# Whole low parts in the feed-forward networks, a third pair in seven products, and later small tables in a two-layer trunk

## The chip, the cores and the metric

The kernel runs on one core of a Trainium2 chip. The metric is the time on the device in microseconds (us), the median of several runs. The names of the engines are those of the profile: PE is TensorE (matrix products), PEld its loading of weights, DVE is VectorE, ACT is ScalarE, POOL is GpSimd and SP is SyncE, which here only starts transfers (DMAs).

## What is computed

A decoder trunk of two layers, forward over 256 positions (one batch) of width 2048, in float32. Layer 0 mixes by an mLSTM (8 heads) beside a Mamba-2 scan (32 heads), with one projection in front of both and one behind; layer 1 mixes by block-sparse attention. Behind each mixer stands a SwiGLU network with 5632 hidden units. Cut to what matters:

```python
def swiglu(x, w_gate, w_up, w_down):
    return (jax.nn.silu(x @ w_gate) * (x @ w_up)) @ w_down

for layer in range(DEPTH):
    xn = rms_norm(x, norm_mix[layer])
    if layer % 2 == 0:
        x = x + mixer_mlstm_ssd(xn, *mixer_params[layer])
    else:
        x = x + mixer_moba(xn, *mixer_params[layer])
    x = x + swiglu(rms_norm(x, norm_ffn[layer]), *ffn_params[layer])
return rms_norm(x, final_norm)
```

## The kernel before, in words

**High and low parts.** To keep the accuracy of float32, each weight and each activation is split in two: a high part, which ScalarE makes by a cast to the matmul's format (line 441, `wh`), and a low part, what is left, which VectorE makes by a subtraction (line 443, `wl`). Each product of a 128x128 block of activations with a 128x512 block of weights is three matmuls: high by high (line 475), activation high by weight low (line 476), and activation low by weight high (line 477). Line 476 alone needs `wl`. In the mixer's projections the same is done in the lines 383 and 387 from the splits of lines 367 and 368.

**Blocks.** `block` computes 256 tokens by 1024 columns, over pairs of 128 rows of the weight. One pair is one *unit* of weights: a DMA of 512 KB on SyncE's queue into `raw`, 128 partitions by 4x512 numbers. `weights` casts and subtracts a unit in two halves of 128x1024. A string says of each pair how it is computed: P is a plain pair, 8 products or 24 matmuls; S is a pair *in seven products* (a Strassen form), 21 matmuls. For S, VectorE also makes sums of weights (lines 450, 451 and 453, into `sums`), which are split as a second unit, and only three quarters of the raw unit are split (128x1536). Sums of activations (`sk`) are made by `sums_of`. The matmuls of one S pair go over the banks `acc_f` (four results) and `acc_e` (the products that several results share).

**The feed-forward network.** `ffn` makes 11 strips of 512 hidden units in groups of 4, 4 and 3. `hidden` makes a strip: a block of gate and up columns, then Silu (line 1011), the product (line 1012), and 128x128 transposes of the strip on TensorE. Some strips are first copied by a DMA from GpSimd's queue into `hr`, a tile in the matmul's format, and transposed from there (line 282); the others are transposed as plain float32 (line 284). Behind each group come two blocks of `w_down` (`add_blocks`, the halves q of the columns), whose plans are in `PLAN_H`; their results are added to the residual (line 909). The network of layer 0 is a, that of layer 1 is b, so `ha` and `hb` are their hidden units.

**Order.** The kernel is written operation by operation, and a scheduler places each on its engine by priority (`high_priority` with an offset) and by what it needs; `issue_after` ties one to another. Steps that are put off, transposes and parts of the mixer, go into a list with a number of steps to wait (`later`, `transpose_later`), and `tick` runs what is due behind a product. An engine then carries out its instructions in the order in which they stand. Units are staged in rings of three buffers each for `raw`, `wh` and `wl`, with an extra `raw`.

**The start.** `keep_busy(11)` gives TensorE 11 small matmuls of float32, which the profile shows as 22, until the first x and the first weights are there. x comes in features by tokens on SyncE's queue (`first_x`, `xraw`), the first two 128-row blocks of weights as two transfers, one from ScalarE's queue and one from SyncE's. Small tables (`ident`, `pv`, `alog`, `gbias`, `d_bc`, `mask_sl`) come from GpSimd's queue, and `cw_rows` from ScalarE's. Further on in the mixer, gate columns are transposed into `p_cols` (line 690).

Of the kernel before, what the change touches and what calls it, by code (L numbers as in the profile page):

```python
# [9 lines left out]
F32 = mybir.dt.float32  # L10
# [7 lines left out]
P = 128  # L18
# [22 lines left out]
PLAN_H = {4: ("PSPSPPPP", "PSPSPSPP"), 3: ("PSPSPP", "PSPSPP")}  # L41
# [24 lines left out]
def hybrid_trunk(ctx: ExitStack, tc: tile.TileContext, a: dict, out: bass.AP):  # L66
# [121 lines left out]
    keep_busy(11)  # L188
# [15 lines left out]
    nc.gpsimd.dma_start(alog[32:64], col1(a["l0_ssd_a_log"]))  # L204
    ident_r = cst.tile([P, P], F32R, name="ident_r")
    ident = ident_r.bitcast(F32)
    ident_in = t2([P, P], "ident_in")
    nc.gpsimd.dma_start(ident_in, a["ident"])
    nc.gpsimd.dma_start(ident, ident_in)
# [11 lines left out]
    def split(h, l, src, gain=None):  # L221
        if gain is None:
            nc.scalar.copy(h, src)
            nc.vector.tensor_sub(l, src, h.bitcast(F32))
        else:
            nc.scalar.activation(h, src, AF.Copy, scale=gain)
            nc.vector.scalar_tensor_tensor(l, src, gain, h.bitcast(F32), op0=OP.mult, op1=OP.subtract)
# [124 lines left out]
    def chunks(w, col, nk, first=KC):  # L352

        n = 4 if staging else KC
        for k in range(0, nk, KC):
# [4 lines left out]
            step = KC if k else first  # L360
            for i in range(0, KC, step):
                ks = slice(k % n + i, k % n + i + step)
                eng = nc.scalar if step < KC and i == 0 else nc.sync
                eng.dma_start(raw[:, ks, :],
                              w[(k + i) * P:(k + i + step) * P, col:col + STRIP].rearrange("(a p) f -> p a f", p=P))
                with tc.high_priority(offset=800):
                    nc.scalar.copy(wh[:, ks, :], raw[:, ks, :])  # L367
                    nc.vector.tensor_sub(wl[:, ks, :], raw[:, ks, :], wh[:, ks, :].bitcast(F32))  # L368
            ks = slice(k % n, k % n + KC)
            yield k, wh[:, ks, :], wl[:, ks, :]  # L370

    def lin_w(w, col, kt, nk, ready=None):
# [5 lines left out]
        for k0, wh, wl in chunks(w, col, nk, KC if ready is None else 1):  # L378
# [49 lines left out]

    def weights(src, row, summed):
# [7 lines left out]
        def parts(of, cuts):  # L437
# [4 lines left out]
            for c in cuts:  # L442
# [121 lines left out]

    def input_ready(k, last):

        if k % 2 == 0 and k < KD:
            if k == 0:
                nc.gpsimd.dma_start(pv, a["columns"])
            if k + 2 < KD:  # L570
                load_x(k + 2)
            for j in (k, k + 1):
                h, l = xt0.block(k // 4)[:, j % 4, 0, :], xt0.block(k // 4)[:, j % 4, 1, :]
                with tc.high_priority(offset=750 if j > 1 else 2000):
                    x = first_x[:, KD + j * T:KD + (j + 1) * T] if j < KC else xraw[2 * k // KD][:, j % (KD // 2), :]
                    split(h, l, x, first_x[:, j:j + 1])
# [3 lines left out]
    banks_q = lin_w(w_in, C_Q, xt0, KD, ready=input_ready)  # L580
# [3 lines left out]
    for t in range(NT):  # L584
        nc.gpsimd.dma_start(xin[t], x_in[t * P:(t + 1) * P, :])
    gbias = cst.tile([96, 1], F32, name="gbias")
    nc.gpsimd.memset(gbias, 0.0)
    nc.gpsimd.dma_start(gbias[0:8], col1(a["l0_mlstm_gate_bias"][8:16]))
    nc.gpsimd.dma_start(gbias[32:64], col1(a["l0_ssd_dt_bias"]))
    nc.gpsimd.dma_start(gbias[64:72], col1(a["l0_mlstm_gate_bias"][0:8]))  # L590
    d_bc = cst.tile([P, SH], F32, name="d_bc")
    dsrc = a["l0_ssd_d"]
    nc.gpsimd.dma_start(d_bc, bass.AP(tensor=dsrc.tensor, offset=dsrc.offset, ap=[[0, P], [1, SH]]))
    mask_sl = cst.tile([P, P], F32, name="mask_sl")
    nc.gpsimd.dma_start(mask_sl, a["mask_sl"])
# [4 lines left out]
    with tc.issue_after(emptied[1].ins):  # L600
        nc.vector.tensor_scalar(convw, cw_rows, 0.5, None, op0=OP.mult)
        nc.vector.tensor_scalar(convb, pv[:, G_CB:G_CB + 32], 0.5, None, op0=OP.mult)
# [4 lines left out]
    with tc.issue_after(emptied[0].ins):  # L607
        nc.scalar.activation(lam, alog, AF.Exp)
# [614 lines left out]
```

## Time and profile before

| what | value |
|---|---|
| median of 3 runs | 2559.82 us (2558.21 to 2562.22) |
| the profiled execution | 2558.07 us |
| its span | 2556.3 us |
| granted TensorE clock, mean | 0.999 |
| TensorE busy | 99% of the span, 12179 matmuls |
| VectorE busy | 85%, 2679 instructions |
| ScalarE busy | 57% |
| GpSimd busy | 2% |
| DMA | 509.58 MB, mean 199 GB/s |

In the timeline a row is: start, duration, engine, line, operation, output from inputs, shape, and how many such are in the row; a bracket gives the idle time ahead and what ended it. In a table of waits a row says which engine waited at which output for what: us in total, times, the longest. In groups by line, a row has the busy time, the mean of one in ns, and the idle time just ahead with what ended it. Matmuls overlap with the next one, so what counts is the distance of their starts and not their duration.

### The profile page before, as it was taken

The numbers are of one execution on the slowest core, as the hardware profiler recorded it, in microseconds if no ns is written. First come the engines' busy times: TensorE is split into PE (matmuls) and PEld (weight loads), VectorE is DVE, ScalarE is ACT, GpSimd is POOL, SyncE is SP. The second block draws the span as 40 slices with busy tenths as digits, with TensorE's granted clock in tenths as the row PEclk, the third lists the DMA queues.
The fourth block names the chain that finished last, engine by engine and source line by source line (L and its number), as shares of the span: only waits on it lengthen the run. The fifth ranks groups of instructions, "written<-read, shape, count | busy, mean of one in ns | idle before, by whom it ended". The sixth has DMA issues, their size and how long they took to land.

```text
span 2556.3 us, 32504 instructions
## 1 busy us (share of the span) xinstructions
PE 2541.2 (99%) x12179; PEld 2129.6 (83%) x12179; DVE 2176.5 (85%) x2679; ACT 1465.2 (57%) x1940; POOL 59.7 (2%) x112
## 2 busy tenths in 40 slices
PE   9999999999999999999999999999999999999998
PEld 8888888888888888888888888888888888888887
DVE  5776778798989998999899987767999988998898
ACT  6465665566556554555455655666665545564554
POOL 1000010000000000000000000000000000000000
PEclk9999999999999999999999999999999999999999
DMA  8665576566565666566656556554556756575754
GB/s 281 181 209 185 165 231 185 167 204 214 181 214 182 217 212 202 200 222 216 196 200 212 196 172 230 165 165 149 196 184 213 234 177 222 198 239 167 236 190 165
DMA packets 257774, 509.58 MB, mean 199 GB/s; under 512 B 16232, under 2 KB 16512, under 8 KB 257104
## 3 DMA queue, kind: packets, MB, share of 16 engines
q1 hardware_dynamic: 249952, 483.20, 58.0%
q0 software_dynamic: 6224, 21.56, 2.4%
q10 hardware_dynamic: 1440, 2.75, 0.3%
q8 instruction: 95, 1.56, 0.2%
q14 instruction: 63, 0.52, 0.1%
HBM read 494.76 MB, written 2.14 MB: 194 GB/s over the span
## 4 chain that ended last, share of the span: by engine, by line
PE 94%; DVE 3%; issue 1%; DMA 1%; ACT 1%; SPq 0%; POOLq 0%; POOL 0%; DVEq 0%; ACTq 0%
PE acc_f L475 19%; PE acc_f L476 18%; PE acc_f L477 18%; PE acc_w L383 11%; PE acc_w L387 6%; PE acc_e L475 4%; PE acc_e L477 4%; PE acc_e L476 4%; PE acc_a L413 2%; PE acc_a L414 2%; PE acc_a L415 2%; PE p_y L872 1%; PE p_tr L284 1%; DVE wl L443 1%; DMA raw<-in_l_w_o 1%
## 5 line engine op out<-in xcount | busy, mean ns | idle before, releaser
L441 ACT CAST wh<-raw 128x1024 fp32r<-128x1024 f32 (+1 forms) x573 | 628.6, 1137 | 496.7 <-PE acc_f L477 384.1
L443 DVE TENSOR_TENSOR wl<-raw,wh 128x1024 fp32r<-128x1024 f32 (+1 forms) x573 | 745.8, 1327 | 119.2 <-ACT wh L441 115.8
L475 PE MATMUL acc_f<-wh,x 128*128 128x512 f32 x1122 | 438.6, 391 | 0.5 <-DVE xres L909 0.5
L477 PE MATMUL acc_f<-wh,x 128*128 128x512 f32 x1122 | 436.9, 389 | 0.0
L476 PE MATMUL acc_f<-wl,x 128*128 128x512 f32 x1122 | 436.6, 389 | 0.0
L368 DVE TENSOR_TENSOR wl<-raw,wh 128x1024 fp32r<-128x1024 f32 (+1 forms) x225 | 271.0, 1217 | 130.5 <-ACT wh L367 126.8
L441 ACT CAST wh<-sums 128x1024 fp32r<-128x1024 f32 x230 | 234.8, 1051 | 199.7 <-PE acc_f L477 137.4
L367 ACT CAST wh<-raw 128x1024 fp32r<-128x1024 f32 (+1 forms) x225 | 231.7, 1044 | 184.4 <-PE acc_w L383 94.4
L443 DVE TENSOR_TENSOR wl<-sums,wh 128x1024 fp32r<-128x1024 f32 x230 | 273.6, 1219 | 11.9 <-ACT wh L441 11.7
L477 PEld LDWEIGHTS acc_f<-wh,x 128*128 128x128 f32 x1122 | 210.6, 188 | 44.1
L475 PEld LDWEIGHTS acc_f<-wh,x 128*128 128x128 f32 x1122 | 210.6, 188 | 43.8 <-issue 0.9
L476 PEld LDWEIGHTS acc_f<-wl,x 128*128 128x128 f32 x1122 | 210.6, 188 | 43.0
L383 PE MATMUL acc_w<-xa,wh 128*128 128x512 f32 x768 | 207.9, 398 | 2.9 <-ACT wh L367 1.9
L383 PEld LDWEIGHTS acc_w<-xa,wh 128*128 128x128 f32 x768 | 139.2, 189 | 29.1 <-ACT wh L367 3.3
L450 DVE TENSOR_TENSOR sums<-raw 128x1024 f32<-128x1024 f32 x115 | 140.2, 1219 | 23.0 <-DMA raw<-in_l_ffn_up 11.3
L383 PE MATMUL acc_w<-x,wh 128*128 128x512 f32 x512 | 139.2, 399 | 0.0
L387 PE MATMUL acc_w<-xa,wl 128*128 128x256 f32 x768 | 121.1, 282 | 0.0
L387 PEld LDWEIGHTS acc_w<-xa,wl 128*128 128x128 f32 x768 | 109.6, 190 | 6.5
L383 PEld LDWEIGHTS acc_w<-x,wh 128*128 128x128 f32 x512 | 92.4, 189 | 16.9
L475 PE MATMUL acc_f<-wh,hb 128*128 128x512 f32 (+1 forms) x272 | 105.1, 387 | 0.0
L477 PE MATMUL acc_f<-wh,hb 128*128 128x512 f32 (+1 forms) x272 | 105.1, 386 | 0.0
L476 PE MATMUL acc_f<-wl,hb 128*128 128x512 f32 (+1 forms) x272 | 105.1, 386 | 0.0
(354 smaller groups left out, 4567.9 us busy)
## 6 DMA issues: line engine op xcount, KB each, us to landing
raw<-in_l_w_in SPq DMA_DIRECT2D x191, 512.0 KB, 3.7
raw<-in_l_ffn_gate SPq DMA_DIRECT2D x176, 512.0 KB, 3.9
raw<-in_l_ffn_up SPq DMA_DIRECT2D x176, 512.0 KB, 4.8
raw<-in_l_ffn_down SPq DMA_DIRECT2D x176, 512.0 KB, 5.1
raw<-in_l_w_qkv SPq DMA_DIRECT2D x96, 512.0 KB, 4.6
raw<-in_l_w_out SPq DMA_DIRECT2D x64, 512.0 KB, 5.1
raw<-in_l_w_o SPq DMA_DIRECT2D x32, 512.0 KB, 4.7
hr<-h POOLq DMA_DIRECT2D x40, 256.0 KB, 4.0
```

Of the source, the lines that this page charges most:

```text
L367: nc.scalar.copy(wh[:, ks, :], raw[:, ks, :])
L368: nc.vector.tensor_sub(wl[:, ks, :], raw[:, ks, :], wh[:, ks, :].bitcast(F32))
L383: return nc.tensor.matmul(banks[f], wh[:, kk, f * P:(f + 1) * P], kt.both(k0 + kk), start=k0 + kk == 0, stop=False, skip_group_check=True)
L387: nc.tensor.matmul(banks[f][:, :T], wl[:, kk, f * P:(f + 1) * P], kt.parts(k0 + kk)[0], start=False, stop=k0 + kk == nk - 1, skip_group_ch ...
L413: nc.tensor.matmul(banks[t], xh[:, ts], wh[:, kk, :], start=k0 + kk == 0, stop=False)
L414: nc.tensor.matmul(banks[t], xh[:, ts], wl[:, kk, :], start=False, stop=False)
L441: nc.scalar.copy(h[:, c, :], of[:, c, :])
L443: nc.vector.tensor_sub(l[:, c, :], of[:, c, :], h[:, c, :].bitcast(F32))
L450: nc.vector.tensor_sub(sums[:, 0:2, :], raw[:, 2:4, :], raw[:, 3:0:-2, :])
L475: nc.tensor.matmul(dst, ah, bh, start=start, stop=False)
L476: nc.tensor.matmul(dst, ah, bl, start=False, stop=False)
L477: nc.tensor.matmul(dst, al, bh, start=False, stop=stop)
```

## The change

**A third S pair.** The plan of the first down block behind a group of four strips, one of "PSPSPPPP", becomes "PSPSPSPP". There are two such blocks in each network. The sums of activations for that pair are made three steps earlier.

**Whole low parts.** Within `ffn` a unit's low part is one subtraction of 128x2048 (128x1536 for the raw unit of an S pair, as before) in place of two of 128x1024; the casts stay in halves. That is 264 units.

**The last strip of a group** is never copied by GpSimd: 8 copies fewer, and 32 transposes go from line 282 to line 284. They are due one step sooner.

**The start.** One idle matmul fewer; ScalarE casts the first x, then the first weights, then the second x, then the second weights, and the subtractions of the weights come behind both. The small tables and `cw_rows` are loaded by GpSimd's queue behind the large loads of x in rows (`xin0`, `xin1`). What is worked out from them (`convw`, `convb`, `lam`) is done behind the second strip of q.

**The mixer.** The gate columns' transposes are put off by four steps, the adding of the mask to the decay rows by two.

The core of the diff:

```diff
-PLAN_H = {4: ("PSPSPPPP", "PSPSPSPP"), 3: ("PSPSPP", "PSPSPP")}
+PLAN_H = {4: ("PSPSPSPP", "PSPSPSPP"), 3: ("PSPSPP", "PSPSPP")}
...
-    keep_busy(11)
+    keep_busy(10)
...
+            if k == 0 and lead is not None:
+                for i, eng in enumerate((nc.scalar, nc.sync)):
+                    eng.dma_start(raw[:, i, :], rows[:, i, :])
+                with tc.high_priority(offset=2000):
+                    for i in range(KC):
+                        with tc.issue_after(cast.ins) if i else nullcontext():
+                            xh, xl = lead(i)
+                        with tc.issue_after(xh.ins):
+                            cast = nc.scalar.copy(wh[:, i, :], raw[:, i, :])
+                with tc.high_priority(offset=800), tc.issue_after(xl.ins):
+                    for i in range(KC):
+                        nc.vector.tensor_sub(wl[:, i, :], raw[:, i, :], wh[:, i, :].bitcast(F32))
...
-            for c in cuts:
+            for c in (slice(0, cuts[-1].stop),) if whole_lows[0] else cuts:
                 nc.vector.tensor_sub(l[:, c, :], of[:, c, :], h[:, c, :].bitcast(F32))
...
-    nc.scalar.dma_start(cw_rows, a["conv_w_columns"])
+    with tc.issue_after(xin_loads[0].ins):
+        nc.gpsimd.dma_start(cw_rows, a["conv_w_columns"])
+        nc.gpsimd.dma_start(pv, a["columns"])
+        nc.gpsimd.dma_start(alog[32:64], col1(a["l0_ssd_a_log"]))
+        nc.gpsimd.dma_start(ident_in, a["ident"])
+    with tc.issue_after(xin_loads[1].ins):
+        nc.gpsimd.dma_start(ident, ident_in)
...
+    later(4, "cols", turn_cols)
...
+            later(2, ("hm", s), masked, mrows[0])
...
         first = 0
+        whole_lows[0] = True
         for n in (4, 4, 3):
             hT = KT(f"h{name}{first}", 4 * n)
-            hT.sums = summed(PLAN_H[n][0])
+            hT.sums = {1: None, 3: None}
             for i in range(n):
-                hidden(hT, i, first + i, PLAN_X if first + i else PLAN_LATE, n == 4 or i < n - 1)
+                hidden(hT, i, first + i, PLAN_X if first + i else PLAN_LATE, i < n - 1)
...
-                       ahead=(((5, sums_of, hT, 5, False),) if n == 4 else (), ()))
+                       ahead=(((2, sums_of, hT, 5, False),) if n == 4 else (), ()))
             first += n
+        whole_lows[0] = False
```

Three places at which the order moves. The first is TensorE's queue in the last down block of network b, at its first S pair (banks `acc_e` and `acc_f`; a number behind a name is that of the tile, and `wl` has the number of its `wh` and one more). Before:

```order
L477 MATMUL acc_f_20678<-wh_20710,skh_20037 128x512
L475 MATMUL acc_e_20727<-wh_20710,hb80_20020 128x512
L476 MATMUL acc_e_20727<-wl_20711,hb80_20020 128x512
L477 MATMUL acc_e_20727<-wh_20710,hb80_20020 128x512
L475 MATMUL acc_e_20731<-wh_20715,skh_20037 128x512
L476 MATMUL acc_e_20731<-wl_20716,skh_20037 128x512
L477 MATMUL acc_e_20731<-wh_20715,skh_20037 128x512
```

Now, at the same place (the lines 475, 476 and 477 have become 480, 481 and 482, and the tiles have other numbers):

```order
L482 MATMUL acc_e_20470<-wh_20454,hb80_19780 128x512
L480 MATMUL acc_e_20474<-wh_20459,skh_19797 128x512
L480 MATMUL acc_e_20478<-wh_20459,skh_19797 128x512
L480 MATMUL acc_e_20482<-wh_20459,skh_19797 128x512
L480 MATMUL acc_f_20435<-wh_20459,hb80_19780 128x512
L480 MATMUL acc_f_20422<-wh_20492,hb81_20099 128x512
L480 MATMUL acc_e_20470<-wh_20527,hb81_20099 128x512
L481 MATMUL acc_e_20474<-wl_20460,skh_19797 128x512
```

Before, each product's three matmuls stand together. Now six matmuls that need a high part alone stand ahead of the first that reads the low part `wl_20460`; `wh_20492` is the next plain unit, and `wh_20527` the next S unit.

The second is VectorE's queue at that place. Before:

```order
L443 TENSOR_TENSOR wl_20711<-raw_20704,wh_20710 128x1536
L453 TENSOR_TENSOR sums_20707<-raw_20704,sums_20707 128x512
L443 TENSOR_TENSOR wl_20716<-sums_20707,wh_20715 128x1024
L443 TENSOR_TENSOR wl_20750<-raw_20746,wh_20749 128x1024
L443 TENSOR_TENSOR wl_20716<-sums_20707,wh_20715 128x1024
L443 TENSOR_TENSOR wl_20750<-raw_20746,wh_20749 128x1024
L450 TENSOR_TENSOR sums_20782<-raw_20779 128x1024
```

Now:

```order
L458 TENSOR_TENSOR sums_20451<-raw_20448,sums_20451 128x512
L1176 TENSOR_TENSOR xres0_4817<-xres0_4817,gf_20159 128x512
L455 TENSOR_TENSOR sums_20524<-raw_20521 128x1024
L1176 TENSOR_TENSOR xres1_4818<-xres1_4818,gf_20159 128x512
L448 TENSOR_TENSOR wl_20460<-sums_20451,wh_20459 128x2048
L448 TENSOR_TENSOR wl_20493<-raw_20489,wh_20492 128x2048
L456 TENSOR_TENSOR sums_20524<-raw_20521,sums_20524 128x512
```

Before, halves of the two units alternate, and the sum for the next S pair comes behind them. Now each low part is one row, and that sum and two additions of the output's residual stand ahead of the first.

The third is GpSimd's queue at the start. Before:

```order
L203 MEMSET alog_129 64x1
L208 DMA ident_in_133<-in_ident 128x128
L204 DMA alog_129<-in_l0_ssd_a_log 32x1
L213 MEMSET mhalf_136 128x16
L569 DMA pv_126<-in_columns 128x128
L587 MEMSET gbias_378 96x1
L593 DMA d_bc_383<-in_l0_ssd_d 128x32
```

Now, from the first load of x in rows on:

```order
L591 DMA xin0_368<-in_x 128x2048
L600 DMA cw_rows_376<-in_conv_w_columns 128x128
L601 DMA pv_125<-in_columns 128x128
L602 DMA alog_128<-in_l0_ssd_a_log 32x1
L603 DMA ident_in_377<-in_ident 128x128
L591 DMA xin1_369<-in_x 128x2048
L605 DMA ident_r_130<-ident_in_377 128x128
```

The tables, which stood at the queue's head, now stand behind `xin0` and `xin1`.

More of the change, by code (lines that the diff above doesn't have):

```diff
@@ L1 @@
-from contextlib import ExitStack
+from contextlib import ExitStack, nullcontext
 import numpy as np
@@ L350, in row_norm, with chunks @@
         return r, rb
[L352 removed]
+    def chunks(w, col, nk, lead=None):
         n = 4 if staging else KC
@@ L359, in chunks @@
                 wl = unit("wl", [P, n, STRIP], "wl", F32R)
[L360 to L365, printed above, removed]
+            rows = w[k * P:(k + KC) * P, col:col + STRIP].rearrange("(a p) f -> p a f", p=P)
+            ks = slice(k % n, k % n + KC)
+            if k == 0 and lead is not None:
[10 more added lines that the diff above has]
+                        nc.vector.tensor_sub(wl[:, i, :], raw[:, i, :], wh[:, i, :].bitcast(F32))
+            else:
+                nc.sync.dma_start(raw[:, ks, :], rows)
                 with tc.high_priority(offset=800):
@@ L563, in hybrid_trunk, with split_x, first_pair @@
     ss0 = cst.tile([P, NT, 4], F32, name="ss0")
+    def split_x(j, x):
+        return split(xt0.block(j // 4)[:, j % 4, 0, :], xt0.block(j // 4)[:, j % 4, 1, :], x, first_x[:, j:j + 1])
+    def first_pair(j):
+        return split_x(j, first_x[:, KD + j * T:KD + (j + 1) * T])
     def input_ready(k, last):
         if k % 2 == 0 and k < KD:
-            if k == 0:
-                nc.gpsimd.dma_start(pv, a["columns"])
             if k + 2 < KD:
                 load_x(k + 2)
[L572 to L576, printed above, removed]
+            for j in range(max(k, KC), k + 2):
+                with tc.high_priority(offset=750):
+                    split_x(j, xraw[2 * k // KD][:, j % (KD // 2), :])
     qT = long([P, MH, T], "qT")
     kT = long([P, MH, T], "kT")
-    banks_q = lin_w(w_in, C_Q, xt0, KD, ready=input_ready)
+    banks_q = lin_w(w_in, C_Q, xt0, KD, input_ready, first_pair)
     for f in range(4):
@@ L617, in hybrid_trunk @@
                 emptied = lin_sum(banks[f], qT[:, 4 + f, :])
+            with tc.issue_after(emptied[1].ins):
+                nc.vector.tensor_scalar(convw, cw_rows, 0.5, None, op0=OP.mult)
+                nc.vector.tensor_scalar(convb, pv[:, G_CB:G_CB + 32], 0.5, None, op0=OP.mult)
+            with tc.issue_after(emptied[0].ins):
+                nc.scalar.activation(lam, alog, AF.Exp)
+            with tc.issue_after(emptied[1].ins):
+                nc.vector.tensor_scalar(lam, lam, -1.0, None, op0=OP.mult)
             continue
```

54 lines of the change are left out of this document (22 added, 32 removed).

## The prediction

> **What bounds the kernel now.** First the profile page's busy shares and its chain of waits:
>
> ```profile
> PE 2541.2 (99%) x12179; PEld 2129.6 (83%) x12179; DVE 2176.5 (85%) x2679; ACT 1465.2 (57%) x1940; POOL 59.7 (2%) x112
> PE 94%; DVE 3%; issue 1%; DMA 1%; ACT 1%; SPq 0%; POOLq 0%; POOL 0%; DVEq 0%; ACTq 0%
> ```
>
> TensorE (PE) is the bound: busy 99% of the span, 94% of the chain that ended last. VectorE (DVE), at 85%, has the least room of the rest. So I read next what TensorE waits for, which is all that an edit elsewhere could win:
>
> ```profile
> PE acc_w L383 <- ACT wh L367: 1.9, 1, 1.9
> PE p_idle L186 <- POOL alog L203: 1.0, 1, 1.0
> PE acc_w L383 <- DVE xa L227: 1.0, 1, 1.0
> PE acc_f L475 <- DVE xres L909: 0.5, 1, 0.5
> PE p_cols L690 <- ACT colsrc L681: 0.4, 1, 0.4
> PE p_tr L284 <- DVE pre L528: 0.3, 1, 0.3
> ```
>
> These six waits are 5.1 us of 2556. Little is to be won by hiding things; time moves by TensorE's own work, and by new waits. The profiled execution took 2558.07 us (span 2556.3); the median of three runs is 2559.82. I sum against the former and add the difference, 1.75, at the end. A measurement of this kernel can tell about 0.2%, some 5.1 us, from no change.
>
> **Third pair in seven products.** The order shows 2637 matmuls for each of lines 475 to 477 where there were 2641: four blocks each lose one product, 3 matmuls, so 12. Their pitch:
>
> ```profile
> 2520.13 0.39 PE L475 MATMUL acc_f<-wh,hb 128*128 128x512 f32 x1
> 2522.17 0.39 PE L475 MATMUL acc_e<-wh,skh 128*128 128x512 f32 x1
> ```
>
> Nine matmuls start from 2520.13 to 2522.17, 0.227 us each, so 12 give **-2.7**. [...]
>
> VectorE pays for it. One such block before, and the costs of its operations:
>
> ```profile
> 966.80:1009.00 42.20, 42.20 (x188) 34.94 (x188) 34.71 (x33) 19.00 (x19) 0.00 (x0) 1.00 0.51 162
> L443 DVE TENSOR_TENSOR wl<-raw,wh 128x1024 fp32r<-128x1024 f32 x458 | 546.5, 1219 | 103.2 <-ACT wh L441 100.4
> L443 DVE TENSOR_TENSOR wl<-raw,wh 128x1536 fp32r<-128x1536 f32 x115 | 201.6, 1753 | 16.0 <-ACT wh L441 15.4
> L453 DVE TENSOR_TENSOR sums<-raw,sums 128x512 f32<-128x512 f32 x115 | 78.8, 685 | 1.0
> ```
>
> The window's columns after the length are the busy times of PE, weight loads, DVE, ACT, POOL. A plain pair has two subtractions of 1.22. A pair in seven products has one of 1.75, a sum of 1.22, two of 0.69, and two more subtractions of 1.22: about 4.3 us more, 4.0 where neighbours overlap. VectorE then has some 38 to 39 us to do in 41.5, ahead of the saving below. It fits as a total; what decides is when each low part comes.
>
> **Low parts by whole units.** A width of 512 takes 0.685 us, 1024 takes 1.219, 1536 takes 1.753: 0.534 for each 512, so 2048 would take 2.29 (an estimate), 0.15 less than two halves. Over 264 units that is 40 us of VectorE's 2176, nearly all of it off the path. The price is that the first half of a low part, usable after 1.22 us, now comes after 2.29, and that the subtraction can begin only when both halves' casts are done. TensorE cannot start the low product before. I walked three sorts of place.
>
> *A block of four strips, first half (four blocks).* Before:
>
> ```profile
> 940.32 0.39 PE L475 MATMUL acc_f<-wh,ha 128*128 128x512 f32 x1
> 940.52 1.22 DVE L1008 TENSOR_TENSOR pre<-pre,acc_f 128x1024 f32<-128x1024 f32 x1
> 941.66 2.36 DVE L443 TENSOR_TENSOR wl<-sums,wh 128x1024 fp32r<-128x1024 f32 x2
> 943.94 1.22 DVE L450 TENSOR_TENSOR sums<-raw 128x1024 f32<-128x1024 f32 x1
> 945.07 0.68 DVE L224 TENSOR_TENSOR ha<-p_tr,ha 128x512 fp32r<-128x512 f32 x1
> 945.67 0.68 DVE L451 TENSOR_TENSOR sums<-raw,sums 128x512 f32<-128x512 f32 x1
> 946.27 0.75 DVE L1012 SCALAR_TENSOR_TENSOR h<-pre,r,h 128x512 f32<-128x512 f32 x1
> ```
>
> By the starts, a 1024-wide operation occupies VectorE for 1.14 us, a 512-wide one for 0.60. In the new order VectorE does, from 940.52 on: the add (1.14), two 512-wide sums (1.2), a 1024-wide sum (1.14), a whole low part (2.2), a 512-wide split (0.6), line 1012 (0.67), another 512-wide one (0.6) and the next whole low part (2.2): 9.75 in all, to about 950.3. TensorE, from 940.32 on, has 33 matmuls (7.5), a pair of transposes and nine matmuls whose operands need no low part (2.0), and stands at about 950.0. That is a stall of 0.35; the second such pair's low part of the sums, behind the split of the last strip and the sums of the activations on VectorE, comes about 0.6 late. So 0.95 for a block, 3.8 for four.
>
> *The last block of the second network's hidden units.* Before:
>
> ```profile
> 2523.53 0.39 PE L475 MATMUL acc_e<-wh,skh 128*128 128x512 f32 x1
> 2523.88 0.50 PE L476 MATMUL acc_e<-wl,skh 128*128 128x512 f32 x1
> 2522.28 2.42 ACT L441 CAST wh<-raw 128x1024 fp32r<-128x1024 f32 x2
> ```
>
> TensorE has a gap here: 0.35 between starts where the pitch is 0.23. Now six matmuls with the high part alone stand ahead of the first low product (the change's section has the rows). The sixth reads the next pair's high part, whose 1536-wide cast is the later of the two ending at 2524.70. TensorE is there after nine and five matmuls from 2520.13, at 2523.3, and waits 1.4, against which the gaps of before go: **+1.25**. In the order, all later matmuls stand behind it.
>
> *Hidden strips where a DMA is late (eight places).*
>
> ```profile
> DVE sums L450 <- DMA raw<-in_l_ffn_up: 11.3, 8, 2.4
> 913.95 1.22 DVE L450 TENSOR_TENSOR sums<-raw 128x1024 f32<-128x1024 f32 x1 [1.55 <-DMA raw<-in_l_ffn_up]
> 916.96 4.02 DVE L443 TENSOR_TENSOR wl<-raw,wh 128x1024 fp32r<-128x1024 f32 x3
> 918.71 0.39 PE L476 MATMUL acc_f<-wl,x 128*128 128x512 f32 x1
> ```
>
> The three 916.96 subtractions are two halves of a unit and the first of the next. TensorE's low product at 918.71 reads the first half, ready at 918.18 (916.96 and 1.22). A whole low part would be ready at 919.25 (916.96 and 2.29), 0.54 late, some 4 over the eight. But how late the transfer is differs among the eight, and the wait of 1.55 here is above their mean of 1.4, so I take nothing and keep 4 for the bound. Two blocks of three strips, not walked, would add up to 1.2 each.
>
> So the new waits: walked places in full, 3.8 + 1.25 = **+5.0**; upper bound 11.5 with the others; lower bound -1, which is the next paragraph.
>
> **What VectorE's relief may win.** In the chain that ended last, the end of the program goes through VectorE:
>
> ```profile
> 2521.46 0.98 DVE wl L443
> 2523.74 1.22 DVE wl L443
> ```
>
> Six such units at 0.15 would be 0.9 sooner if VectorE sets the end. I leave it at nothing in the sum.
>
> **The start.**
>
> ```profile
> 1.00 4.10 PE L186 MATMUL p_idle<-ones 128*128 128x128 f32 x22 [1.00 <-POOL alog L203]
> 6.05 2.12 PE L383 MATMUL acc_w<-xa,wh 128*128 128x512 f32 x8 [0.95 <-DVE xa L227]
> 9.92 1.04 ACT L367 CAST wh<-raw 128x1024 fp32r<-128x1024 f32 x1 [1.95 <-DMA raw<-in_l_w_in]
> 11.02 2.12 PE L383 MATMUL acc_w<-xa,wh 128*128 128x512 f32 x8 [1.91 <-ACT wh L367]
> DMA packets 1897, 3.11 MB, mean 259 GB/s; under 512 B 336, under 2 KB 480, under 8 KB 1897
> q0 software_dynamic: 267, 0.25, 12.8%
> cw_rows<-in_conv_w_columns ACTq DMA_DIRECT2D x1, 64.0 KB, 4.8
> ```
>
> The second weight unit lands at 9.92, and TensorE waits 1.9 for its cast. In the first 12 us the small tables (queue q0 0.25 MB, cw_rows 0.06) share the transfers; they now go behind the big x loads. 0.31 MB at 259 GB/s is 1.2 us, so that unit lands some 1.2 earlier. Putting each x cast ahead of its weight cast lets TensorE begin up to 0.5 earlier, but the second unit is what ends last, so this only counts if that is early too. I take **-1.3**; bounds 0 (the queue shares otherwise) and -2.4 (both). Idle pairs drop from 11 to 10, some 0.37 us less ahead of 6.05, which no wait hangs on unless the clock does (below). The column transposes come four steps later, past their cast: **-0.4**. The masks, convw and lam are needed later than their tables land; they cost nothing beside 85% of VectorE; late, they would hold one operation of the mixer, at the price of the nearest row, 0.4 for p_cols.
>
> **Last strips without copy.**
>
> ```profile
> L282 PE MATMUL p_tr<-ident_r,hr 128*128 128x128 f32 x160 | 15.9, 243 | 0.0
> L284 PE MATMUL p_tr<-ident_r,xres 128*128 128x128 f32 x96 | 12.2, 273 | 0.3 <-DVE pre L528 0.3
> ```
>
> 15.9/160 is 0.099 for a transpose of the copied form, 12.2/96 is 0.127 for the plain one; 32 change over: **+0.9**. Eight copies on POOL's queue vanish; POOL is 2% busy, so that wins nothing. The transposes come one step sooner in four strips; were line 1012 late for them, each could cost what the last wait of TensorE's table did, 0.3. The groups of three strips do without the copy already, and the table has no such wait for them, so nothing.
>
> **The sum.** -2.7 + 5.0 - 1.3 - 0.4 + 0.9 = +1.5: 2559.6 for the profiled execution, **2561.3** against the median.
>
> **The rivals.**
> *Slower: a matmul held by a late cast or low part.* All places that I bounded come in, 11.5, and the start gains nothing: -2.7 + 11.5 - 0.4 + 0.9 = +9.3, so 2569. For it: TensorE's order is fixed, and the walk found waits at two of three sorts of place. Against: the table of TensorE's waits has no row for a low part of line 443 before, so there is some room, and matmuls with the high part alone now stand ahead of the low products and bridge. It decides once the new waits pass 8.6. Chance 0.21. [...]
> *Faster: no new wait.* VectorE, 40 us lighter, is never late; the start wins its most; the end 0.9: -2.7 - 2.4 - 0.4 + 0.9 - 0.9 = -5.5, so 2554.3. For it: VectorE stands idle 100.4 us of the span for casts ahead of these subtractions (the first row by width above), so it often has time. Against: the walks. Chance 0.21.
> *The clock.* With ten idle pairs the clock could still be throttled at 6.05.
>
> ```profile
> 0.00:10.00 10.00, 7.16 (x38) 6.42 (x38) 3.06 (x6) 4.52 (x9) 6.05 (x27) 1.00 0.82 230
> ```
>
> Before, it is granted at 1.00 throughout; at half speed the first eight matmuls would take 2.12 more, of which what is left of the wait of 1.9 behind them, 0.7, hides a part: at most +1.4, 2562.7. Chance 0.06. [...]
> That the change does not do what it says is excluded: the order shows 12 matmuls fewer.
>
> **Chances.** My forecast 0.52 (0.47 within 0.2%, 0.03 slower, 0.02 faster), slower rival 0.21, faster rival 0.21, clock 0.06 (within). That gives faster 0.23, same 0.53, slower 0.24. The range goes from 2553.0, inside the faster rival's spread, to 2570.0, just past the slower one.
>
> **What would show it.** In the profile after: 12 matmuls fewer; whole low parts of 2.29; rows of waits of TensorE for wl at line 448 in the first down blocks of four strips, near 0.3 to 0.6 each, and one of some 1.4 near the end for a cast; the wait of 1.9 at the second weight unit reduced to about 0.7; transposes from h at 0.127. It is wrong if TensorE's waits for lows in sum are under 1 us (then the faster rival), or over 8.6 (the slower one).

## The result, and the profile after

The changed kernel takes 2579.64 us (median of four runs, 2577.63 to 2580.90), the kernel before 2560.03 (four runs): ratio 1.0076, interval 1.0064 to 1.0088. It is 0.76% slower, some 19.6 us, where 2561.3 was forecast and 2570.0 was the end of the range. The profiled execution has a span of 2575.9 us, 19.6 more than before. The page's busy shares and chain of the changed kernel:

```profile
PE 2550.7 (99%) x12165; PEld 2125.8 (83%) x12165; DVE 2171.4 (84%) x2431; ACT 1472.9 (57%) x1944; POOL 55.7 (2%) x105
...
PE 83%; DVE 9%; DMA 3%; issue 3%; ACT 2%; SPq 0%; DVEq 0%; POOLq 0%; POOL 0%; ACTq 0%
```

The busy shares hide the loss: TensorE is at 99% as before, because a matmul's row lasts 0.39 where the next starts 0.227 behind it, so that a gap of under 0.16 does not show. The chain points to it: TensorE held 94% of it, now 83%, and VectorE, DMA and ScalarE have taken 9, 3 and 2. Its shares are no measure of the loss, though: TensorE has 92% in a run further down that takes 2575.95 us and 76% in one of 2562.14. What TensorE waits for, changed kernel:

```profile
PE acc_f L481 <- DVE wl L448: 6.6, 10, 1.4
PE acc_e L481 <- DVE wl L448: 2.0, 5, 0.7
PE acc_e L480 <- ACT wh L446: 1.9, 4, 1.3
PE p_tr L278 <- DVE pre L533: 1.6, 1, 1.6
PE p_idle L186 <- POOL alog L203: 1.0, 1, 1.0
PE acc_w L386 <- DVE xa L221: 0.7, 1, 0.7
PE acc_f L480 <- DVE xres L929: 0.7, 2, 0.4
PE p_cols L706 <- ACT colsrc L693: 0.4, 1, 0.4
```

The first three rows are new and make 10.5 us, 8.6 of it for low parts. Starts of the same matmuls in both traces say where: in the last projection of layer 0's mixer the changed kernel is 1.5 us ahead (516.34 and 514.88); in the first mixer strip of layer 1 it is 11.7 behind (1606.34 and 1618.07), so network a, with the seam into it, lost 13.2; the mixer of layer 1 adds nothing (1762.01 and 1773.72); the last matmul starts 20.1 later (2546.30 and 2566.36), so the seam into network b and b itself lost 8.4.

The largest stall of the hidden strips, in network a. Timeline of the changed kernel, with VectorE, SyncE's issue of the load, and TensorE:

```profile
819.47 0.75 DVE L1032 SCALAR_TENSOR_TENSOR h<-pre,r,h 128x512 f32<-128x512 f32 x1
...
820.73 3.96 DVE L448 TENSOR_TENSOR wl<-raw,wh 128x2048 fp32r<-128x2048 f32 x2
823.05 0.37 SPq L439 DMA_DIRECT2D raw<-in_l_ffn_gate  x1
823.46 0.47 SPq L439 DMA_DIRECT2D raw<-in_l_ffn_up  x1
...
830.16 1.23 DVE L455 TENSOR_TENSOR sums<-raw 128x1024 f32<-128x1024 f32 x1 [2.50 <-DMA raw<-in_l_ffn_up]
...
832.76 3.95 DVE L448 TENSOR_TENSOR wl<-raw,wh 128x2048 fp32r<-128x2048 f32 x2
833.33 0.39 PE L480 MATMUL acc_f<-wh,x 128*128 128x512 f32 x1
835.10 0.50 PE L481 MATMUL acc_f<-wl,x 128*128 128x512 f32 x1 [1.38 <-DVE wl L448]
```

VectorE idles 2.50 us at the sums of the next S pair, whose load is late. The low part of the plain pair, for which TensorE will wait, is queued behind these sums. It begins at 832.76, is whole at 835.05, and TensorE, due at 833.56, goes on at 835.10: 1.54 us. The same place with the low parts in halves and all else of the change kept (the first experiment), where TensorE stands 1.03 us earlier:

```profile
818.84 2.35 DVE L448 TENSOR_TENSOR wl<-raw,wh 128x1024 fp32r<-128x1024 f32 x2
821.11 0.75 DVE L1032 SCALAR_TENSOR_TENSOR h<-pre,r,h 128x512 f32<-128x512 f32 x1
821.22 0.37 SPq L439 DMA_DIRECT2D raw<-in_l_ffn_gate  x1
821.63 1.18 SPq L439 DMA_DIRECT2D raw<-in_l_ffn_up  x1
...
828.09 1.23 DVE L455 TENSOR_TENSOR sums<-raw 128x1024 f32<-128x1024 f32 x1 [2.30 <-DMA raw<-in_l_ffn_up]
...
830.69 4.02 DVE L448 TENSOR_TENSOR wl<-raw,wh 128x1024 fp32r<-128x1024 f32 x3
...
832.52 0.39 PE L481 MATMUL acc_f<-wl,x 128*128 128x512 f32 x1
```

From the sums on, VectorE has the same operations in the same order. The first half is ready at 831.91 (830.69 and 1.22), 0.61 ahead of its use at 832.52. So TensorE has 0.61 us of slack here. Against that clock (1.03 added), the load was issued 0.80 later in the changed kernel (823.46 against 822.66) and the sums began 1.04 later (830.16 against 829.12); the low part then took 1.07 more to the first use (2.29 against 1.22). 1.04 and 1.07, less 0.61, is 1.50: the stall. Either delay alone would have cost 0.4 to 0.5.

Why was the load issued later? What SyncE waits for in the changed kernel (window 815 to 825):

```profile
SPq L439 <- DVE wl L448: 13.6, 2, 10.6
```

Its two transfers for a unit, gate and up columns, go out when the subtraction that uses the buffer is done: at 823.05 behind 823.02 (820.73 and 2.29), and with halves at 821.22 behind 821.19 (818.84 and 2.35). A whole subtraction thus took no longer here than two halves in a row (2.29 and 2.35). But it began 0.86 later by TensorE's clock (820.73 against 819.87). Of this, 0.66 is the product of line 1032, which the scheduler has put ahead of it and which stands behind it with halves; the rest was not followed. So at this place the buffer came free later by VectorE's new order, and not by the length of the subtraction.

In the last down block, six matmuls with the high part stand ahead, and the sixth waits for a cast, as walked in the prediction:

```profile
2541.02 2.29 DVE L448 TENSOR_TENSOR wl<-sums,wh 128x2048 fp32r<-128x2048 f32 x1
...
2541.43 0.63 PE L480 MATMUL acc_f<-wh,hb 128*128 128x512 f32 x2
2543.32 0.50 PE L480 MATMUL acc_e<-wh,hb 128*128 128x512 f32 x1 [1.26 <-ACT wh L446]
```

The two of the second row start at 2541.43 and 2541.66, so the sixth was due at 2541.89: 1.43 us, where 1.4 was forecast. None of the matmuls that stand behind it in the queue starts ahead of it; the next starts at 2543.66. The low part of the first row, which the next matmul reads, was ready at 2543.31, no earlier than the cast. The prediction's walk had not seen that: without the late cast the low part alone would have held its matmul, due at 2542.12, for 1.2. In the first down block of four strips:

```profile
951.51 0.39 PE L480 MATMUL acc_e<-wh,ha 128*128 128x512 f32 x1
952.04 0.50 PE L481 MATMUL acc_f<-wl,ha 128*128 128x512 f32 x1
952.38 0.40 PE L482 MATMUL acc_f<-wh,ha 128*128 128x512 f32 x1
...
961.95 0.61 PE L480 MATMUL acc_f<-wh,ha 128*128 128x512 f32 x2
962.97 0.50 PE L481 MATMUL acc_e<-wl,skh 128*128 128x512 f32 x1 [0.41 <-DVE wl L448]
```

Two stalls: 0.31 (0.53 between 951.51 and 952.04, less 0.227) and 0.57 (the second of the two at 961.95 starts at 962.18, so the next was due at 962.40). The third row shows a detail that recurs behind each of the 15 waits of `acc_f` and `acc_e` for a low part in the table above: the matmul that waited lasts 0.50 and the next starts 0.34 behind it (0.335 to 0.340, once 0.386) in place of 0.227.

At the seam into network b, VectorE of the changed kernel:

```profile
1851.91 2.29 DVE L448 TENSOR_TENSOR wl<-raw,wh 128x2048 fp32r<-128x2048 f32 x1 [0.70 <-ACT wh L446]
1854.12 0.68 DVE L532 TENSOR_TENSOR pre<-pre,acc_e 128x512 f32<-128x512 f32 x1
1854.71 0.68 DVE L533 TENSOR_TENSOR pre<-pre,acc_e 128x512 f32<-128x512 f32 x1
```

A whole low part for the network's first strip idles 0.70 for its second cast, runs 2.29, and has the last two sums of the attention's output behind it, on which the transposes of the residual wait 1.6 us. This place lies outside the network's own blocks.

### The profile page after: what moved, and what is told of

The parts are those of the page before. It is cut to its first block, busy times and chain, and to the rows that moved or that the text cites. A ratio compares the mean times of both kernels' runs of the same rounds, so it can differ in the third digit from the quotient of the medians.

```text
span 2575.9 us, 32308 instructions
## 1 busy us (share of the span) xinstructions
PE 2550.7 (99%) x12165; PEld 2125.8 (83%) x12165; DVE 2171.4 (84%) x2431; ACT 1472.9 (57%) x1944; POOL 55.7 (2%) x105
## 4 chain that ended last, share of the span: by engine, by line
PE 83%; DVE 9%; DMA 3%; issue 3%; ACT 2%; SPq 0%; DVEq 0%; POOLq 0%; POOL 0%; ACTq 0%
PE acc_f L481 16%; PE acc_f L482 16%; PE acc_f L480 15%; PE acc_w L386 11%; PE acc_w L390 6%; DVE wl L448 4%; PE acc_e L481 3%; PE acc_e L482 3%; PE acc_e L480 3%; PE acc_a L416 2%; PE acc_a L417 2%; PE acc_a L418 2%; DMA raw<-in_l_ffn_up 2%; DMA raw<-in_l_ffn_down 1%; DVE sums L455 1%
## 5 line engine op out<-in xcount | busy, mean ns | idle before, releaser
L446 ACT CAST wh<-raw 128x1024 fp32r<-128x1024 f32 (+1 forms) x569 | 626.8, 1140 | 430.1 <-PE acc_f L482 340.0
L448 DVE TENSOR_TENSOR wl<-raw,wh 128x2048 fp32r<-128x2048 f32 (+2 forms) x401 | 724.7, 1827 | 118.8 <-ACT wh L446 79.6
L446 ACT CAST wh<-sums 128x1024 fp32r<-128x1024 f32 x238 | 245.2, 1051 | 257.3 <-PE acc_f L482 145.3
L372 DVE TENSOR_TENSOR wl<-raw,wh 128x1024 fp32r<-128x1024 f32 x223 | 269.7, 1223 | 127.7 <-ACT wh L371 123.9
L371 ACT CAST wh<-raw 128x1024 fp32r<-128x1024 f32 x223 | 230.7, 1048 | 181.5 <-PE acc_w L386 96.0
L448 DVE TENSOR_TENSOR wl<-sums,wh 128x2048 fp32r<-128x2048 f32 (+1 forms) x142 | 275.3, 1944 | 37.8 <-ACT wh L446 37.6
L455 DVE TENSOR_TENSOR sums<-raw 128x1024 f32<-128x1024 f32 x119 | 145.3, 1221 | 20.0 <-DMA raw<-in_l_ffn_up 12.6
L481 PE MATMUL acc_f<-wl,ha 128*128 128x512 f32 x256 | 100.8, 394 | 1.8 <-DVE wl L448 1.4
L481 PE MATMUL acc_e<-wl,skx 128*128 128x512 f32 x261 | 101.7, 390 | 0.0
```

Source lines behind the costliest of these rows:

```text
L446: nc.scalar.copy(h[:, c, :], of[:, c, :])
L448: nc.vector.tensor_sub(l[:, c, :], of[:, c, :], h[:, c, :].bitcast(F32))
L455: nc.vector.tensor_sub(sums[:, 0:2, :], raw[:, 2:4, :], raw[:, 3:0:-2, :])
L481: nc.tensor.matmul(dst, ah, bl, start=False, stop=False)
```

## The experiments

The times in this section are medians; each stands beside runs of the kernel before on the same chip, whose medians were 2558.05 to 2559.13. Differences between two runs are of the medians as they stand; where the kernel before had different medians beside them (2560.03 in the result), up to 2 us of a difference may come from that.

**Halves again.** Of the changed kernel, one line is left out:

```diff
-        whole_lows[0] = True
```

> The change, with each low part in the feed-forward networks again in two halves of 128x1024 where the raw unit is not cut to 1536. Theory L (whole low parts cost nearly all: the first half comes 1.1 us later and the raw buffer is freed later, so that the next load, and the sums behind it on VectorE, come later too): the loss of 20 us goes, 2555 to 2559 us, and TensorE has no row of waits for wl at line 448. Theory P (the third pair's extra work makes VectorE late, and the lateness is carried on in its queue): at least 10 us of the loss stay, 2568 to 2576 us. Theory T (most of it is the transposes and the rest of the change): 2575 us or more.

2556.72 us, ratio 0.9991 (0.9983 to 1.0000): the whole loss is gone. The waits of TensorE in this kernel:

```profile
PE p_idle L186 <- POOL alog L203: 1.0, 1, 1.0
PE acc_f L481 <- DVE wl L448: 0.8, 1, 0.8
PE acc_f L480 <- DVE xres L929: 0.5, 1, 0.5
```

One row for low parts is left, 0.8 us at the seam into b. Theory L stands, P and T fall. Whole low parts cost 22.9 us within the change (2579.64 less 2556.72).

**Two S pairs again, with whole low parts.**

```diff
-PLAN_H = {4: ("PSPSPSPP", "PSPSPSPP"), 3: ("PSPSPP", "PSPSPP")}
+PLAN_H = {4: ("PSPSPPPP", "PSPSPSPP"), 3: ("PSPSPP", "PSPSPP")}
...
-            hT.sums = {1: None, 3: None}
+            hT.sums = summed(PLAN_H[n][0])
...
-                       ahead=(((2, sums_of, hT, 5, False),) if n == 4 else (), ()))
+                       ahead=(((5, sums_of, hT, 5, False),) if n == 4 else (), ()))
```

> The change, with the plan of the first down blocks of four strips back to two pairs in seven products and the sums of activations made as before; whole low parts stay. Theory L: the stalls of hidden strips stay (5 us in network a) and those of the down blocks shrink; 2573 to 2580 us. Theory P: 2560 to 2566 us. Theory T: 2578 us or more.

2583.84, ratio 1.0096 (1.0081 to 1.0112): outside what each theory gave but T's "2578 or more", and T had just fallen. The third pair is no cause; without it the loss is 4 us larger. In the profiled execution (2585.19, the slowest of four) some 3 us of that are the clock, at the start and at the seam into b (both below).

**Both undone.**

> The change, with both undone: halves again and two pairs in seven products; what is left is the start, the later tables and masks, and the last strips that are not copied. Theories L and P: 2557 to 2561 us (by the traces the start won 1.5 us and plain transposes cost 0.9). Theory T: 2570 us or more.

2558.52, ratio 0.9998 (0.9989 to 1.0007), as expected by L and P. With the two runs above: the third pair wins 1.8 us with halves (2558.52 to 2556.72; 2.7 was forecast); whole low parts cost 25.3 without the third pair; the rest of the change makes no difference that can be told (0.6).

**Whole low parts for the sums alone, for the raw units alone.**

```diff
-            for c in (slice(0, cuts[-1].stop),) if whole_lows[0] else cuts:
+            for c in (slice(0, cuts[-1].stop),) if whole_lows[0] and of is not raw else cuts:
```

> The change, with whole low parts for the units of sums alone (96); the 168 raw units have halves again. Whole lows cost 23 us in all. If each whole low part costs alike, 96 of 264 units give 8 us: 2564 to 2566. If TensorE has some slack at each place, which only the sum of several delays uses up (a coarser low part, and a load that starts later), the part costs much less than its share: 2557 to 2561. If the sums are what does it, since the second half of an S pair hangs on them, 2570 or more.

> The change, with whole low parts for the 168 raw units alone; sums have halves. If each costs alike, 168 of 264 give 15 us: 2570 to 2573. With the slack, less than the share: 2560 to 2567. If raw units do it alone, since a raw buffer that is freed later puts off the next load, 2576 to 2580.

2562.79 (ratio 1.0013) and 2575.58 (1.0064). Each lies between the intervals of two cases: the sums between a slack and an equal price, the raw units between an equal price and "raw units do it alone". Against 2556.72 these are 6.1 for 96 units and 18.9 for 168, 25.0 together where both at once cost 22.9. So the parts add up to within some 2 us, and the theory of a slack that only several delays use up is not borne out as a rule over the whole kernel, though the place above has it. A raw unit costs 0.11 us, a unit of sums 0.06: raw units cost nearly twice as much.

**Whole low parts in the hidden strips alone, in the down blocks alone.** `whole_lows` is set and cleared around `hidden` or around `add_blocks`.

> The change, with whole low parts in the blocks of the hidden strips alone, halves in the down blocks. By the profile of the change, the stalls over 0.12 us in hidden strips are 4.8 us in network a and 0.2 in b, and those at the seam into b some 2.2: 2562 to 2566. If the lateness in the hidden strips comes over from the down blocks ahead of them: 2557 to 2560.

> The change, with whole low parts in the down blocks alone, halves in the hidden strips. If the places add up, it takes what the run with the hidden strips alone left of the 23 us: 2556.7 and 9.3, so 2564 to 2568. If the lateness is carried over from hidden strips into down blocks, 2558 to 2562.

2570.32 (1.0043) and 2565.82 (1.0032): 13.6 and 9.1, together 22.7. The places add up, as the second run expected. The hidden strips, in which the seam into b is counted, cost more than the 7 us that the first expectation read from the stalls of the changed kernel.

**Pieces of 128x512.**

```diff
-            for c in (slice(0, cuts[-1].stop),) if whole_lows[0] else cuts:
+            for c in [slice(i, i + 1) for i in range(cuts[-1].stop)] if whole_lows[0] else cuts:
```

> The change, with low parts in pieces of 128x512, four of them to a unit (three to the raw unit of an S pair), in place of whole ones. VectorE has some 0.53 us a unit more to do than with wholes by the widths' steps of 0.534 and the fixed part of 0.15. If what costs is how late the first rows of a low part come, this is as good as halves: 2555 to 2559. If VectorE's total work sets the time, it is worse than halves: 2565 or more.

2559.17, ratio 1.0000 (0.9991 to 1.0009): the finest pieces are 2.4 us behind halves and 20 ahead of wholes, although VectorE has most to do with them (busy 2234.3 us, where wholes have 2171.4). VectorE's total work did not set the time.

**The sums behind the plain pair's low part.** The first sum of an S pair is issued after the low part of the plain pair ahead of it:

```diff
+            with nullcontext() if plain_low[0] is None else tc.issue_after(plain_low[0].ins):
+                nc.vector.tensor_sub(sums[:, 0:2, :], raw[:, 2:4, :], raw[:, 3:0:-2, :])
```

> The change, whole low parts and all, with the first sum of an S pair's weights put on VectorE behind the low part of the plain pair ahead of it. If whole low parts cost because they stand behind sums whose load is late (VectorE waits for a DMA with a low part queued behind), the five stalls in the hidden strips of network a (4.8 us, and a few tenths behind them) go, and 2570 to 2575 us are left; with the stalls in the down blocks that have the same queue, down to 2566. If it is the width alone (the first rows come 1.1 us later wherever the low part stands), it stays at 2577 to 2582. If the sums, now later, are late for their own products, more than 2582.

2572.77, ratio 1.0057 (1.0044 to 1.0070): 7 us better, in the first case's interval. The waits of TensorE now:

```profile
PE acc_e L484 <- DVE wl L449: 4.6, 5, 1.2
PE acc_f L484 <- DVE wl L449: 2.3, 1, 2.3
```

Of the ten waits at `acc_f` in the changed kernel, five in the hidden strips of network a among them, one is left, at the seam into b. In their place TensorE waits longer for the sums' own low parts (`acc_e`, 0.82 or 0.83 in each first down block of four strips, where it was 0.16 to 0.66). The queue's order is a part of the loss, and turning it round moves a part of it to the third theory's place.

**A fifth raw buffer.** The FFN stage gets a second spare raw buffer; for its 8 KB a partition the pool of small tiles shrinks, also in the yardstick:

```diff
-FFN = ({"rawx": 1}, {"skh": 3}, {"blk": 4}, {"pre": 1})
+FFN = ({"rawx": 2}, {"skh": 3}, {"blk": 4}, {"pre": 1})
...
-    tmp = ctx.enter_context(tc.tile_pool(name="tmp", bufs=9))
+    tmp = ctx.enter_context(tc.tile_pool(name="tmp", bufs=5))
...
-            if turn["spare"] % 4 == 3:
+            held_ = [tags["rawx"] for _, tags in stage["pools"] if "rawx" in tags][0]
+            if turn["spare"] % (3 + held_) >= 3:
```

> The change with whole low parts and a fifth buffer for raw units in the feed-forward networks; for its room the pool of small tiles has 5 buffers in place of 9, as in the next run, beside which this is read. If loads that start later, since a whole low part frees its raw buffer later, are what makes it slow, this wins at least 5 us on the next run. If not, within 3 us of it.

> The change with whole low parts and 5 buffers in the pool of small tiles in place of 9, the raw buffers as they are: the yardstick for the run before. 2579 to 2590 us by both theories.

2567.20 (1.0035) beside 2581.86 (1.0094) in the yardstick: 14.7 us. The place shown above, with the fifth buffer (SyncE's issue, then VectorE):

```profile
819.72 0.51 SPq L440 DMA_DIRECT2D raw<-in_l_ffn_up  x1
...
824.94 1.22 DVE L456 TENSOR_TENSOR sums<-raw 128x1024 f32<-128x1024 f32 x1
...
831.12 3.96 DVE L449 TENSOR_TENSOR wl<-raw,wh 128x2048 fp32r<-128x2048 f32 x2 [1.43 <-PE acc_e L483]
```

The load is issued at 819.72 and no wait for a DMA stands ahead of the sums; the low part waits for a matmul instead (as I read it, for a free `wl` buffer), and TensorE does not wait here. VectorE's order is not the same either: the first sum now stands ahead of the sums' low part of the pair before. So this run does not separate the fifth buffer from the order that the scheduler makes with it.

**Is it a cure for whole low parts, or for anything?** The fifth buffer with halves, and four buffers with halves, both with 5 small tiles:

> The change with halves, the fifth raw buffer and 5 small tiles. If the fifth buffer only takes away the delay that whole low parts bring, halves win nothing by it: 2556 to 2560. If halves too wait for loads, they win as well: 2548 to 2553.

> The change with halves, four raw buffers and 5 small tiles. If the fifth buffer does nothing for halves, 2560 to 2564, as with it; then whole low parts cost 20 us with four raw buffers and 5 with five. If halves gain by it as well, 2570 or more.

2562.14 (1.0012, 1.0003 to 1.0021) and 2556.96 (0.9991, 0.9982 to 1.0000). This table, all with 5 small tiles, settles it:

| | halves | whole low parts | whole costs |
|---|---|---|---|
| four raw buffers | 2556.96 | 2581.86 | 24.9 |
| five raw buffers | 2562.14 | 2567.20 | 5.1 |

The fifth buffer does not help halves; it costs them 5 us, which no case expected of these two runs allowed for and whose cause was not looked for. With it, whole low parts cost 5 us in place of 25. So most of their cost, about 20 us, hangs on the number of raw buffers and on the order that comes with it.

**Both cures.**

> Whole low parts with both cures: the sums of a pair behind the plain pair's low part, and the fifth raw buffer with 5 small tiles. If the two cures act on the same stalls (a load that starts late, and a low part queued behind it), it is near the fifth buffer alone, 2564 to 2568. If they act on different ones, they add up (7 and 14.7 off 2581.9): 2559 to 2562.

2575.95, ratio 1.0068 (1.0055 to 1.0080): neither. The two cures work against each other. With the fifth buffer alone VectorE still waits 8.6 us for loads ahead of sums in the networks (7.0 for up columns, 1.6 for `w_down`), where the changed kernel has 15.7 (12.6 and 3.1). With both cures this wait is gone, but, as I read it, to hold the sums behind a low part delays them by more than it wins (2575.95 beside 2567.20). The waits of TensorE:

```profile
PE acc_e L485 <- DVE wl L450: 5.8, 6, 1.2
PE acc_f L485 <- DVE wl L450: 4.4, 4, 1.5
```

They are for low parts of S pairs in the first row, as with the sums behind alone.

**Whole low parts alone, on the kernel before.**

> The kernel before with whole low parts alone. If they cost what they cost within the change (23 and 25 us, with and without the third pair), 2580 to 2586. If the rest of the change is needed for it, 2560 to 2570.

2574.41, ratio 1.0059 (1.0047 to 1.0072): 15.3 us, between the two expectations. Whole low parts make the kernel slower by themselves, but the rest of the change raises their price by 8 to 10 us. Which part of it does so was not separated. In the profiled execution of this run some 1.5 us of the loss are the clock at the start (last section).

The fastest of all was the change with halves, 2556.72 and, with 5 small tiles, 2556.96: ratios of 0.9991, both with an interval from 0.998 to 1.0000, so a tenth of a per cent ahead of the kernel before, if at all.

## Why the prediction was wrong

**What bounds the kernel** was read rightly: time moved by TensorE's waits (10.5 us of new ones), and VectorE's total did not matter: the run in pieces of 128x512 has the most of it, 2234.3 us, and takes 2559.17.

**The step that failed** is in "Low parts by whole units": "The price is that the first half of a low part, usable after 1.22 us, now comes after 2.29, and that the subtraction can begin only when both halves' casts are done." That is one of two prices. A subtraction also ends the use of a raw buffer, and SyncE's next load waits for that (it went out at 823.05, behind a subtraction that was done at 823.02). With whole low parts the buffer came free later at the place shown, since the subtraction stood later in VectorE's order; the load was issued 0.80 later, the sums of the next S pair began 1.04 later, and the low part for which TensorE waited stood behind these sums. The prediction left every load and, in the hidden strips, VectorE's order where they were in the trace of before. The table by buffers shows the size of this: about 20 of 25 us. That the release through a buffer is the way by which a fifth one helps is shown at one place and agrees with the table; that it is the way at every stall is not shown, and a fifth buffer also changes VectorE's order.

The terms that were too small: for the hidden strips I took nothing and bounded at 4, "0.54 late, some 4 over the eight"; they cost 13.6 when they alone have whole low parts. The second halves of the down blocks were not walked at all: 0.83 of stall in the first group (1006.29 to 1007.35, where 0.227 is due). The seam into b (1.6 for the transposes) was not thought of, since its code lies outside the network; the scheduler brings the network's first low parts forward, in front of the sums that end the attention. The term for new waits was +5.0, at most 11.5; whole low parts cost 22.9.

**What was walked came out.** The last block: 1.43 for 1.4. The first halves of down blocks of four strips: 0.35 and 0.6 were forecast at each; the trace of the changed kernel has 0.31 and 0.57, 0.31 and 0.82 in network a, 0.30 and 0.32, 0.32 and 0.34 in b, in all 3.3 for 3.8. The first of each pair came out every time; the second lies between 0.32 and 0.82, so that the sum fits is in part luck. The walk by hand found the right places where it was made; what was wrong is that places not walked got zero.

**VectorE's operations** took what was estimated. Groups of the changed kernel by shape:

```profile
L448 DVE TENSOR_TENSOR wl<-raw,wh 128x2048 fp32r<-128x2048 f32 x168 | 384.3, 2288 | 91.2 <-ACT wh L446 52.8 <-PE acc_e L482 38.4
L278 PE MATMUL p_tr<-ident_r,h 128*128 128x128 f32 x48 | 7.2, 272 | 0.0
L276 PE MATMUL p_tr<-ident_r,hr 128*128 128x128 f32 x128 | 14.6, 238 | 0.0
```

2.288 for 2.29. Its row shows a second thing: VectorE idles 38.4 us until an `acc_e` matmul is done, which I read as waits for a free `wl` buffer; the row of before named no matmul.

**Last strips without copy.** 7.2/48 is 0.150 for such a transpose and 14.6/128 is 0.114 for the copied form; with 0.099 of before, 32 cost 1.2 to 1.6, more than the 0.9 taken from the transposes of the residual. No run tried it alone.

**Third pair:** -1.8 by the runs for -2.7. The intervals of the two runs (0.9989 to 1.0007 and 0.9983 to 1.0000) are over 4 us wide and cannot tell the two apart.

**The start.** Timeline of the changed kernel:

```profile
0.99 4.62 PE L186 MATMUL p_idle<-ones 128*128 128x128 f32 x20 [0.99 <-POOL alog L203]
6.35 2.10 PE L386 MATMUL acc_w<-xa,wh 128*128 128x512 f32 x8 [0.73 <-DVE xa L221]
...
9.32 2.00 PE L386 MATMUL acc_w<-xa,wh 128*128 128x512 f32 x8
```

And its window over the first 10 us (after the length PE, weight loads, DVE, ACT, POOL, then the granted clock, the DMA share and GB/s):

```profile
0.00:10.00 10.00, 8.27 (x39) 7.39 (x40) 3.82 (x7) 6.24 (x12) 0.96 (x18) 1.00 0.83 272
```

The second unit begins at 9.32 where it was 11.02, and its wait of 1.9 is gone, not only down to 0.7. The first unit begins at 6.35, not earlier than 6.05. Just ahead of the column transposes (121.17 and 119.84) 1.3 are won, as forecast in size, but not by the parts that were added up.

The clock was misread. The window says 1.00 for the first 10 us, as it did before, and the prediction took this for full speed throughout. The starts say otherwise: before, the idle matmuls start 0.21 apart up to 3.93 and 0.11 apart from there; in the changed kernel all 20 start 0.21 apart. Two windows of before count 14 in 2.93 us and 11 in 1.17:

```profile
1.00:3.93 2.93, 2.93 (x14) 2.93 (x15) 0.00 (x0) 1.58 (x2) 2.61 (x7) 1.00 0.71 168
3.93:5.10 1.17, 1.16 (x11) 0.97 (x9) 0.00 (x0) 0.52 (x2) 0.33 (x1) 1.00 1.01 331
```

So in the changed kernel they took 4.62 us, and not 0.37 less than the 4.10 of before, as I had reckoned. I read the step from 0.21 to 0.11 as the clock going from half to full speed. It then came 2.9 us after the first idle matmul before, and more than 4.2 after it here; no run shows what sets the moment. In this execution the clock was up in time for the first unit, whose eight matmuls start some 0.24 apart (the ninth matmul starts at 8.29). In the run with two S pairs and whole low parts, which has the same start, it was not:

```profile
6.17 3.75 PE L386 MATMUL acc_w<-xa,wh 128*128 128x512 f32 x8 [0.53 <-DVE xa L221]
```

Its first unit takes 3.75 for 2.10, with starts 0.43 apart, and the second begins at 10.79, 1.5 later. So the rival of the clock came about there, at about the price that it had (at most 1.4), though not in the changed kernel's profile.

The wait at `p_cols` stayed at 0.4 (last row of the waits), so that term was wrong by 0.4. The steps put into the list did not move the transposes: in both kernels they are the 664th and 665th matmul behind the idle ones, 0.05 behind ScalarE's last write of `colsrc`.

**The rivals.** The slower one had the sign and a part of the mechanism (matmuls held by low parts, at more places than walked), at 2569, 10.6 too low. The condition that it "decides once the new waits pass 8.6" was met, by 10.5 in the table of waits; 0.21 was its chance.

## What to carry to other kernels

An operation that reads a staged buffer has two users: the one that waits for its result (here the matmul at 835.10) and the load that waits for the buffer (here the one that went out at 823.46, 0.80 later than with halves). When such an operation is merged into a longer one, follow both: read where it now stands in its engine's order, and the release in the queue that issues the loads. Before a place gets the price of nothing, walk it, and look also at code next to the change, since a scheduler may put the new long operation ahead of short ones there, as it did with the 2.29 us at 1851.91.

## What the runs showed of the hardware

The granted clock fell in the middle of the kernel in at least three of the profiled runs. In the run with two S pairs and whole low parts, windows at the seam into b (columns: PE, weight loads, DVE, ACT, POOL, then the granted clock, DMA share, GB/s): a pause, 1.4 us at 1.00, the fall, and what follows:

```profile
1856.40:1858.60 2.20, 0.31 (x3) 0.07 (x1) 2.15 (x3) 1.42 (x2) 0.00 (x0) 1.00 0.97 363
1858.60:1860.00 1.40, 1.39 (x12) 1.35 (x13) 0.70 (x1) 1.37 (x3) 0.00 (x0) 1.00 0.17 64
1860.00:1863.40 3.40, 3.40 (x10) 2.63 (x9) 1.99 (x2) 1.96 (x5) 0.00 (x0) 0.50 0.17 30
1863.40:1866.00 2.60, 2.60 (x13) 2.14 (x12) 1.70 (x3) 0.00 (x0) 0.00 (x0) 1.00 1.00 373
```

In the yardstick with few small tiles:

```profile
1867.90:1871.70 3.80, 0.30 (x3) 0.14 (x1) 3.80 (x6) 3.80 (x11) 0.00 (x0) 0.96 0.60 174
1871.70:1874.60 2.90, 2.90 (x7) 2.33 (x8) 2.90 (x5) 2.75 (x8) 0.00 (x0) 0.50 0.99 322
1874.60:1878.00 3.40, 3.40 (x16) 2.73 (x16) 3.40 (x10) 0.62 (x1) 0.00 (x0) 0.97 0.38 148
```

And with the sums behind the low part:

```profile
1863.40:1866.60 3.20, 0.90 (x5) 0.69 (x4) 3.20 (x5) 3.20 (x10) 0.00 (x0) 0.98 0.66 205
1866.60:1869.70 3.10, 3.10 (x8) 2.33 (x8) 3.10 (x9) 2.13 (x5) 0.00 (x0) 0.50 1.03 377
1869.70:1873.00 3.30, 3.30 (x15) 2.72 (x14) 3.30 (x4) 0.25 (x1) 0.00 (x0) 0.97 0.22 84
```

After pauses of 2.2, 3.8 and 2.6 us the clock was granted at 0.50 for about 3.4 us. The windows at 0.50 of the last two runs count 7 matmuls in 2.90 us and 8 in 3.10, where those behind count 16 in 3.40 and 15 in 3.30. At the 0.43 between starts of the slow first unit above, in place of 0.227, seven or eight matmuls lose 1.4 to 1.6 us in all (an estimate). With whole low parts alone on the kernel before it was so at the start: a pause of 2.1 (9.05 to 11.16), then a clock of 0.50 from 12.09 on for 3.4 us. The length of the pause alone did not decide: the kernel before has one of 2.2 at its start (8.83 to 11.02), and the changed kernel one of 1.9 at the seam, and behind both the 512-wide matmuls start 0.23 apart with the clock at 1.00. What decides, no run shows. So behind four pauses of 2.1 to 3.8 us there were, by that estimate, some 1.5 us more to pay, and behind two of 2.2 and 1.9 none.

Behind each of the changed kernel's 15 waits for a low part, one more matmul starts 0.34 behind in place of 0.227, as in the rows of the down block: 0.11 for a stall. In the two networks and the seams into them, the changed kernel has 30 matmuls that start over 0.12 later than 0.227 behind the one ahead, 18.0 us in sum, and with halves 5, 2.4 us; 0.11 for each of 25 more is 2.8. That makes 18.4 of the 21.6 us by which the two profiled spans differ; the rest lies in smaller pieces or elsewhere and was not located.
